# Half of the second row block's normed rows: turned by VectorE 32x32 blocks and a trip through DRAM in place of TensorE

## Chip, core and metric

One core of one Trainium2 chip runs the whole program. The metric is the device time of one execution in microseconds (us). Before the change it is 1993.98 us, the median of three runs (1991.19 to 1994.17).

## What is computed

A decoder layer on 256 tokens of width 2048, in float32: a half-step SwiGLU feed-forward (inner width 5632), a token mixer with two attention branches, a second half-step feed-forward, and a LayerNorm behind each of the three. Only the frame matters here:

```python
h = _layer_norm(ALPHA * h + 0.5 * _swiglu(h, ffn1_w_gate, ffn1_w_up, ffn1_w_down), ln1_g, ln1_b)
mix = _mixer(h, positions, w_in, ...)
h = _layer_norm(ALPHA * h + mix, ln2_g, ln2_b)
return _layer_norm(ALPHA * h + 0.5 * _swiglu(h, ffn2_w_gate, ffn2_w_up, ffn2_w_down), ln3_g, ln3_b)
```

`_layer_norm` takes each row's mean and variance over its 2048 values, and then scales and shifts each column. A matmul on TensorE contracts over partitions, so the normed rows (tokens on the partitions) have to be turned into columns (channels on the partitions) before the next projection can use them.

## The kernel before, in words

**Rows and quads.** The 256 tokens are two blocks of 128 rows, b = 0 and b = 1. The 2048 channels are 16 column tiles of 128, handled in four quads of four tiles (`q` or `c`, 0 to 3); a quad of one block is a 128 x 512 tile. `Acts` holds a turned activation as two float32r tiles, a rounded part `hi` and the rest `lo`. `split` (L148 to L150) makes them: ScalarE copies the source into `hi` (L149), and VectorE subtracts (L150). Each weight tile is loaded by SP's DMA queue and split in the same way into a ring of buffers (`wring`). A product is then three matmuls (`triple`, L202 to L204): hi x hi, hi x lo, lo x hi.

**Order of the work.** `project` (L209) runs over units of two k tiles. A unit is load, split, then 6 matmuls for block 0 and 6 for block 1. The products of block 1 lag behind those of block 0 by `lag` units (`LAG` is 5; `narrow_to` sets it to 1 and shortens the ring). `tick` counts a step per unit, and `later(n, fn)` runs `fn` n steps further on. That is the order in which the program is written; when the kernel is built, a scheduler orders each engine's instructions with its own estimates of their durations. On the chip each engine runs its list strictly in order, and an instruction that waits holds up everything behind it on its engine.

**LayerNorm 1 and 2.** In `LayerNorm.apply(b)` (L604), VectorE computes the factor of a block, then centers and scales each quad in place (L624), and `rows_to_quad` (L498) turns it: four TensorE transposes of 128 x 128 into one PSUM bank (L501), four ScalarE activations with the column's gain and shift from PSUM to SBUF (L506, into `h1raw` or `h2raw` for quads 0 and 1, which are kept for later sums, and into a temporary tile `full` for quads 2 and 3), and `x.put`, which splits. Behind it, twelve and more steps later, `finish` multiplies the rows by the gains and adds the shifts (L629, L630), and GpSimd's DMA queue writes them to DRAM as the next residual (`res<-z`, L1135). LayerNorm 1 runs where the first feed-forward's down projection ends and the mixer's first projections begin (`wc0`, 512 columns; then `narrow_to(6)`, `wc1`, 256 columns, and `wc2`, 320 columns). LayerNorm 2 runs where `w_out` ends and the second feed-forward's gate and up projection begins. In both, the products of block 1's quads 2 and 3 come last among the first projection's products.

**The other way of turning.** `turn_out` (L533) has VectorE transpose a 128 x 512 tile in 32 x 32 blocks (L536), and GpSimd's queue write it with four DMAs of 64 KB to a DRAM tile (L538), so that the blocks land in their turned places. `turn` (L544) reads the tile back with one DMA of 256 KB (L550) into `turned`, `wait` steps after it was written out, and hands it to its user `more` steps after that. In before this way is used for the feed-forward's inner activations and for several of the mixer's tensors, whose column order within a quad is made up for by a host-side order of the weight rows. `blocks`, `turned` and `full` come from one pool of six temporary tiles.

**Where the mixer's key row comes in.** Some 45 us after LayerNorm 1, VectorE makes a rotated key row per block (`kr_row`, L813 to L888), which TensorE turns (L821) amid the first sevenfold products.

Of the kernel before, what the change touches and what calls it, by code (L numbers as in the profile page):

```python
# [14 lines left out]
AF = mybir.ActivationFunctionType  # L15
# [3 lines left out]
P = 128  # L19
# [40 lines left out]
def layer_kernel(ctx: ExitStack, tc: tile.TileContext, a: dict, out: bass.AP):  # L60
    nc = tc.nc
    V, S, GP, PE = nc.vector, nc.scalar, nc.gpsimd, nc.tensor
# [9 lines left out]
    def nm(s):  # L72
        uid[0] += 1
        return f"{s}_{uid[0]}"
# [4 lines left out]
    def tmp_tile(shape, name="tmp", dt=F32):  # L79
        return small.tile(shape, dt, tag="tmp", name=nm(name), bufs=6)  # L80

    def sm(n, name="sm", dt=F32):
        return small.tile([P, n], dt, tag="sm", name=nm(name), bufs=24)
# [4 lines left out]
    def tr_bank(name="tr"):  # L88
        return psum.tile([P, 512], F32, tag="tr", name=nm(name), bufs=3)
# [13 lines left out]
    def later(n, fn):  # L103
        uid[0] += 1
        heapq.heappush(todo, (step[0] + n, uid[0], fn))
# [392 lines left out]
    def rows_to_quad(src, b, x, q, gain=None, shift=None):  # L498
        t = tr_bank()
        for i in range(4):  # L500
            PE.transpose(t[:, i * P:(i + 1) * P], src[:, i * P:(i + 1) * P], ident)  # L501
        if gain is not None:
            full = x.raw(q, b) if q in x.kept else tmp_tile([P, 512], "full")
            for i in range(4):
                k = 4 * q + i
                S.activation(full[:, i * P:(i + 1) * P], t[:, i * P:(i + 1) * P], AF.Identity,  # L506
                             bias=shift[:, k:k + 1], scale=gain[:, k:k + 1])
            t = full
        x.put(q, b, t.rearrange("p (i t) -> p i t", i=4))

    def rstd(v, eps, n, between=None):
        ve = sm(n, "ve")
        V.tensor_scalar(out=ve, in0=v, scalar1=eps, scalar2=None, op0=ALU.add)
        sd = sm(n, "sd")
        S.activation(sd, ve, AF.Sqrt, scale=4.0)
        w = sm(n, "w")
        V.tensor_scalar(out=w, in0=v, scalar1=eps, scalar2=-4.0, op0=ALU.add, op1=ALU.mult)
        if between is not None:
            between()
        y = sm(n, "y")  # L520
        V.reciprocal(y, sd)
        t = sm(n, "t")
        if n == 1:
            V.scalar_tensor_tensor(out=t, in0=y, scalar=w, in1=y, op0=ALU.mult, op1=ALU.mult)
        else:
            y2 = sm(n, "y2")
            V.tensor_tensor(out=y2, in0=y, in1=y, op=ALU.mult)
            V.tensor_tensor(out=t, in0=y2, in1=w, op=ALU.mult)
        f = sm(n, "f")
        V.scalar_tensor_tensor(out=f, in0=t, scalar=3.0, in1=y, op0=ALU.add, op1=ALU.mult)  # L530
        return f

    def turn_out(row, to):  # L533

        t = tmp_tile([P, 512], "blocks")
        V.transpose(t, row)  # L536
        for i in range(4):
            nc.gpsimd.dma_start(to.rearrange("(g r) (i f) -> i r g f", g=4, i=4)[i],  # L538
                                t[32 * i:32 * (i + 1), :].rearrange("r (g f) -> r g f", g=4))

    def turned(v):
        return v.rearrange("p (i k c) -> p k i c", i=4, k=4)

    def turn(row, use, wait, more):  # L544
        to = dram.tile([P, 512], F32, name=nm("turn"))
        turn_out(row, to)

        def back():
            t = tmp_tile([P, 512], "turned")
            nc.gpsimd.dma_start(t, to)  # L550
            later(more, lambda: use(turned(t)))
        later(wait, back)

    def turn_to_quad(row, b, x, q, wait, more):
        turn(row, lambda t: x.put(q, b, t), wait, more)

    def turn_to_cols(row, dst, b, wait, more):
        turn(row, lambda t: S.copy(dst[:, :, b * P:(b + 1) * P].rearrange("p k (i c) -> p k i c", i=4), t), wait, more)

    class LayerNorm:  # L560
        def __init__(self, scale, residual, g, bt, each, x=None, cols=None, at=((0, 2, 4, 6), (8, 11, 14, 17))):
# [42 lines left out]
        def apply(self, b):  # L604
            mv = sm(2, "mv")
            V.bn_aggr(mv, self.stats[b].rearrange("p a s -> p (a s)"))
            zs = [self.z[b][c // 2][:, (c % 2) * 512:(c % 2) * 512 + 512] for c in range(4)]
            gs, bs = ([self.gb[i][c // 2][:, (c % 2) * 512:(c % 2) * 512 + 512] for c in range(4)] for i in range(2))

            if self.cols is None:  # L610
                def center(c):
                    V.scalar_tensor_tensor(out=zs[c], in0=zs[c], scalar=mv[:, 0:1], in1=gs[c],
                                           op0=ALU.subtract, op1=ALU.mult)
                r = rstd(mv[:, 1:2], LN_EPS, 1, lambda: center(0))
                for c in range(4):
                    if c > 0:
                        center(c)
                    V.scalar_tensor_tensor(out=zs[c], in0=zs[c], scalar=r, in1=bs[c],
                                           op0=ALU.mult, op1=ALU.add)
                    self.each(b, c, zs[c])  # L620
                return
            r = rstd(mv[:, 1:2], LN_EPS, 1)
            for c in range(4):
                V.tensor_scalar(out=zs[c], in0=zs[c], scalar1=mv[:, 0:1], scalar2=r,  # L624
                                op0=ALU.subtract, op1=ALU.mult)
                rows_to_quad(zs[c], b, self.x, c, *self.cols)

            def finish(c):
                V.tensor_tensor(out=zs[c], in0=zs[c], in1=gs[c], op=ALU.mult)  # L629
                V.tensor_tensor(out=zs[c], in0=zs[c], in1=bs[c], op=ALU.add)  # L630
                self.each(b, c, zs[c])
            for c in range(4):
                later(12 + c, lambda c=c: finish(c))

    def ffn(n, x, wgu, wdn, residual, g, bt, each, first=None, between=None, nxt=None, cols=None):
# [3 lines left out]
        def put_h(b, q):  # L639
            turn_out(hb[b, q], hT[q, b])  # L640
# [103 lines left out]
    bias = [const.tile([P, 384], F32, name=f"bias{h}") for h in range(DH)]  # L744
# [105 lines left out]
    def mixer(x):  # L850
# [11 lines left out]
        def c_norm(b, i):  # L862
            c = c_row[b][:, i * RANK:(i + 1) * RANK]
            junk = tmp_tile([P, RANK], "junk")
            ss = sm(1, "ss")
            S.activation(junk, c, AF.Square, accum_out=ss)
            ms = sm(1, "ms")
            V.tensor_scalar(out=ms, in0=ss, scalar1=1.0 / RANK, scalar2=None, op0=ALU.mult)
            r = rstd(ms, RMS_EPS, 1)
            V.scalar_tensor_tensor(out=c, in0=c, scalar=r, in1=gain[:, i * RANK:(i + 1) * RANK],  # L870
                                   op0=ALU.mult, op1=ALU.mult)
            turns[i, b] = dram.tile([P, 512], F32, name=nm("turn"))
            later(2, lambda: turn_out(c, turns[i, b]))
# [23 lines left out]
        def cols_proj(w, xx, kt, name, k0=0, more=10):  # L897
            dst = act_tile([P, 4, T], F32, name)

            def done(b, bank):  # L900
                t = tmp_tile([P, 512], name + "r")
                S.copy(t, bank)
                later(1, lambda: turn_to_cols(t, dst, b, 4, more))
            project(w, xx, kt, 512, done, k0)
            return dst
# [16 lines left out]
        def pair_cols(w, name):  # L922
            dst = [act_tile([P, 4, T], F32, name) for _ in range(2)]

            def done(n, b, bank, snap, op):
                t = tmp_tile([P, 512], name + "r")
                V.tensor_tensor(out=t, in0=bank, in1=snap, op=op)
                later(1, lambda: turn_to_cols(t, dst[n], b, 4, 10))
            hy.group(w[0], w[1], done)
            return dst  # L930
# [86 lines left out]
        def qr_done(b, bank):  # L1017
            t = tmp_tile([P, 512], "qr")
            tv = t.rearrange("p (j h i) -> p j h i", j=2, h=MH)
            rope(tv[:, 0], tv[:, 1], bank, b, MH)  # L1020
            later(1, lambda: turn_to_cols(t, qrT, b, 4, 10))
# [193 lines left out]
def _build(arrays):  # L1215
    import numpy as np
    import concourse.bacc as bacc

    nc = bacc.Bacc("TRN2", target_bir_lowering=False, num_devices=1)
    aps = {k: nc.dram_tensor(f"in_{k}_dram", v.shape, mybir.dt.from_np(v.dtype), kind="ExternalInput").ap()  # L1220
           for k, v in arrays.items()}
    out = nc.dram_tensor("out_0_dram", (T, D), F32, kind="ExternalOutput").ap()
    with tile.TileContext(nc) as tc:
        layer_kernel(tc, aps, out)
    return nc
# [9 lines left out]
```

## Time and profile before

| | before |
|---|---|
| median of three runs | 1993.98 us |
| profiled execution | 1992.28 us |
| its span, first to last instruction | 1990.5 us |
| granted TensorE clock, mean | 0.998 of full |
| busy: TensorE, VectorE, ScalarE | 1975.2, 1720.4, 1229.8 us |
| GpSimd, its DMA issues above all | 255.2 us |
| DMA, mean over the span | 233 GB/s |

In the profile, PE is TensorE's matmuls (transposes on TensorE among them), PEld its weight loads, DVE VectorE, ACT ScalarE, POOL GpSimd with its DMA queue, SPq the queue of SyncE. A row of the timeline has start, duration, engine, line, operation, output and inputs, and in brackets how long the engine stood idle before and what it waited for. Durations of matmuls overlap, since they are pipelined: the distance of two starts says what one costs. Lines are those of the kernel before; behind the change the same code lies 4 to 17 lines lower.

### The profile page before, as it was taken

The numbers are of one execution on the slowest core, as the hardware profiler recorded it, in microseconds if no ns is written. First come the engines' busy times: TensorE is split into PE (matmuls) and PEld (weight loads), VectorE is DVE, ScalarE is ACT, GpSimd is POOL, SyncE is SP. The second block draws the span as 40 slices with busy tenths as digits, with TensorE's granted clock in tenths as the row PEclk, the third lists the DMA queues.
The fourth block names the chain that finished last, engine by engine and source line by source line (L and its number), as shares of the span: only waits on it lengthen the run. The fifth ranks groups of instructions, "written<-read, shape, count | busy, mean of one in ns | idle before, by whom it ended". The sixth has DMA issues, their size and how long they took to land.

```text
span 1990.5 us, 25358 instructions
## 1 busy us (share of the span) xinstructions
PE 1975.2 (99%) x8868; PEld 1635.2 (82%) x8868; DVE 1720.4 (86%) x2019; ACT 1229.8 (62%) x1548; POOL 255.2 (13%) x475
## 2 busy tenths in 40 slices
PE   9999999999999999999999999999999999999997
PEld 7888888888888897888888888888888888888886
DVE  7999999999897689999775576799999999987875
ACT  6666666666665566666675754566666666665551
POOL 0111001012110011022130130011110100121000
PEclk9999999999999999999999999999999999999999
DMA  8667756668776666676675686657776666588673
GB/s 326 217 221 267 243 195 211 216 218 264 275 267 225 211 231 235 221 253 231 220 247 187 244 281 227 221 208 238 233 281 204 204 219 234 192 284 294 221 240 110
DMA packets 134607, 463.63 MB, mean 233 GB/s; under 512 B 19616, under 2 KB 19664, under 8 KB 134480
## 3 DMA queue, kind: packets, MB, share of 16 engines
q1 hardware_dynamic: 109296, 389.59, 56.9%
q0 software_dynamic: 25184, 72.43, 11.9%
q8 instruction: 69, 1.13, 0.2%
q14 instruction: 58, 0.48, 0.1%
HBM read 433.11 MB, written 28.84 MB: 232 GB/s over the span
## 4 chain that ended last, share of the span: by engine, by line
PE 94%; DVE 3%; DMA 1%; issue 1%; ACT 0%; SPq 0%; DVEq 0%; ACTq 0%
PE mm L204 30%; PE mm L202 30%; PE mm L203 30%; DVE wring L150 1%; PE tr L202 1%; PE tr L204 1%; PE tr L203 1%; DVE sraw L344 1%; PE tr L501 0%; ACT wring L149 0%; DMA raw<-in_wc_dram 0%; DMA sraw<-in_gu_dram 0%; DMA sraw<-in_wgd_dram 0%; DMA raw<-in_gu_dram 0%; PE tr L1039 0%
## 5 line engine op out<-in xcount | busy, mean ns | idle before, releaser
L150 DVE TENSOR_TENSOR wring<-raw,wring 128x1024 fp32r<-128x1024 f32 (+2 forms) x511 | 612.8, 1204 | 171.6 <-ACT wring L149 165.7
L149 ACT CAST wring<-raw 128x1024 fp32r<-128x1024 f32 (+2 forms) x511 | 529.3, 1040 | 357.7 <-PE mm L204 253.0
L149 ACT CAST wring<-sraw 128x1024 fp32r<-128x1024 f32 x406 | 422.4, 1052 | 195.2 <-PE mm L204 102.3
L202 PE MATMUL mm<-wring,h 128*128 128x512 f32 (+2 forms) x1384 | 534.8, 387 | 0.0
L204 PE MATMUL mm<-wring,h 128*128 128x512 f32 (+2 forms) x1384 | 533.6, 386 | 0.0
L203 PE MATMUL mm<-wring,h 128*128 128x512 f32 (+2 forms) x1384 | 532.6, 385 | 0.0
L150 DVE TENSOR_TENSOR wring<-sraw,wring 128x1024 fp32r<-128x1024 f32 x406 | 487.6, 1219 | 19.2 <-ACT wring L149 14.1
L204 PEld LDWEIGHTS mm<-wring,h 128*128 128x128 f32 x1384 | 260.0, 188 | 52.8 <-DVE h L150 1.4
L203 PEld LDWEIGHTS mm<-wring,h 128*128 128x128 f32 x1384 | 260.0, 188 | 51.6 <-DVE wring L150 0.2
L202 PEld LDWEIGHTS mm<-wring,h 128*128 128x128 f32 x1384 | 260.0, 188 | 51.5 <-ACT h L149 1.0
L203 PE MATMUL mm<-wring,xs 128*128 128x512 f32 x708 | 275.6, 389 | 0.9 <-DVE wring L150 0.9
L202 PE MATMUL mm<-wring,xs 128*128 128x512 f32 x708 | 275.9, 390 | 0.5 <-ACT snap L321 0.5
L204 PE MATMUL mm<-wring,xs 128*128 128x512 f32 x708 | 275.5, 389 | 0.0
L344 DVE TENSOR_TENSOR sraw<-sraw,sraw 128x1024 f32<-128x1024 f32 x200 | 240.8, 1215 | 0.8 <-DMA sraw<-in_gu_dram 0.7
L538 POOL DMA_DIRECT2D hT<-blocks x176 | 95.7, 551 | 760.9 <-DVE blocks L536 708.5
L203 PEld LDWEIGHTS mm<-wring,xs 128*128 128x128 f32 x708 | 132.9, 188 | 28.9 <-DVE wring L150 1.4
L202 PEld LDWEIGHTS mm<-wring,xs 128*128 128x128 f32 x708 | 133.0, 188 | 28.7 <-ACT snap L321 1.0
L204 PEld LDWEIGHTS mm<-wring,xs 128*128 128x128 f32 x708 | 133.0, 188 | 27.4
L203 PE MATMUL mm<-wring,x 128*128 128x512 f32 x384 | 149.6, 390 | 0.5 <-DVE wring L150 0.5
L202 PE MATMUL mm<-wring,x 128*128 128x512 f32 x384 | 149.4, 390 | 0.4 <-ACT wring L149 0.4
L204 PE MATMUL mm<-wring,x 128*128 128x512 f32 x384 | 149.2, 389 | 0.0
L203 PEld LDWEIGHTS mm<-wring,x 128*128 128x128 f32 x384 | 72.1, 188 | 16.1 <-DVE wring L150 1.3
(266 smaller groups left out, 1888.6 us busy)
## 6 DMA issues: line engine op xcount, KB each, us to landing
raw<-in_gu_dram SPq DMA_DIRECT2D x191, 512.0 KB, 4.3
sraw<-in_gu_dram SPq DMA_DIRECT2D x160, 512.0 KB, 5.4
raw<-in_dn_dram SPq DMA_DIRECT2D x144, 512.0 KB, 4.5
hraw<-hT POOLq DMA_DIRECT2D x80, 256.0 KB, 4.9
sraw<-in_dn_dram SPq DMA_DIRECT2D x32, 512.0 KB, 5.4
raw<-in_w_out_dram SPq DMA_DIRECT2D x32, 512.0 KB, 4.4
raw<-in_wgm_dram SPq DMA_DIRECT2D x24, 512.0 KB, 4.5
raw<-in_wgd_dram SPq DMA_DIRECT2D x24, 512.0 KB, 4.2
```

Source lines behind the costliest of these rows:

```text
L149: S.copy(hi, src)
L150: V.tensor_tensor(out=lo, in0=src, in1=hi.bitcast(F32), op=ALU.subtract)
L202: PE.matmul(o, xh, wh, start=first, stop=False, skip_group_check=again)
L203: PE.matmul(o, xh, wl, start=False, stop=False, skip_group_check=again)
L204: PE.matmul(o, xl, wh, start=False, stop=last, skip_group_check=again)
L344: V.tensor_tensor(out=t, in0=t, in1=R[add[1]][s], op=ALU.add)
L538: nc.gpsimd.dma_start(to.rearrange("(g r) (i f) -> i r g f", g=4, i=4)[i], t[32 * i:32 * (i + 1), :].rearrange("r (g f) -> r g f", g=4))
```

## The change

In LayerNorm 1 and 2, quads 2 and 3 of block 1 are no longer turned by `rows_to_quad`. VectorE turns them in 32 x 32 blocks, written in a crossed order (`plain`), so that the tile that comes back holds the columns in their natural order; GpSimd's queue writes each to DRAM with four DMAs and reads it back with one, 2 steps later; and 1 step after that ScalarE applies gain and shift from the tile in SBUF, four column tiles at a time, and `x.put` splits. Block 0, and quads 0 and 1 of block 1, are turned as before. LayerNorm 3 turns nothing.

```diff
-    def turn_out(row, to):
+    def turn_out(row, to, plain=False):
         t = tmp_tile([P, 512], "blocks")
-        V.transpose(t, row)
+        if plain:
+            V.transpose(t.rearrange("p (k g f) -> p g k f", k=4, g=4), row.rearrange("p (g k r) -> p g k r", g=4, k=4))
+        else:
+            V.transpose(t, row)
...
-    def turn(row, use, wait, more):
+    def turn(row, use, wait, more, plain=False):
         to = dram.tile([P, 512], F32, name=nm("turn"))
-        turn_out(row, to)
+        turn_out(row, to, plain)
...
+    def turn_to_scaled(row, b, x, q, gain, shift, wait, more):
+        def use(v):
+            full = tmp_tile([P, 512], "full")
+            for i in range(4):
+                k = 4 * q + i
+                S.activation(full[:, i * P:(i + 1) * P].rearrange("p (i c) -> p i c", i=4), v[:, i], AF.Identity,
+                             bias=shift[:, k:k + 1], scale=gain[:, k:k + 1])
+            x.put(q, b, full.rearrange("p (i t) -> p i t", i=4))
+        turn(row, use, wait, more, True)
...
-                rows_to_quad(zs[c], b, self.x, c, *self.cols)
+                if b == 1 and c >= 2:
+                    turn_to_scaled(zs[c], b, self.x, c, *self.cols, 2, 1)
+                else:
+                    rows_to_quad(zs[c], b, self.x, c, *self.cols)
```

## The prediction

> **What bounds the kernel now.** I read the page first (busy times, then the chain that ended last), and then each engine's timeline where the two LayerNorms turn block 1.
>
> ```profile
> span 1990.5 us, 25358 instructions
> PE 1975.2 (99%) x8868; PEld 1635.2 (82%) x8868; DVE 1720.4 (86%) x2019; ACT 1229.8 (62%) x1548; POOL 255.2 (13%) x475
> ...
> PE 94%; DVE 3%; DMA 1%; issue 1%; ACT 0%; SPq 0%; DVEq 0%; ACTq 0%
> ```
>
> PE is busy 99% of the span and holds 94% of the chain. So a PE instruction that goes is worth its own time at most, and a wait that PE gets costs its full length. Everything else counts only where PE waits for it.
>
> ```profile
> L501 PE MATMUL tr<-ident,z x64: 270/273/328, 692.1 to 1303.5; 128*128 128x128 f32 x64
> ...
> 704.38 0.39 PE L202 MATMUL mm<-wring,h 128*128 128x512 f32 x1
> 704.61 1.47 PE L501 MATMUL tr<-ident,z 128*128 128x128 f32 x12
> 705.84 0.48 PE L203 MATMUL mm<-wring,h 128*128 128x512 f32 x1
> ...
> 706.39 0.40 PE L202 MATMUL mm<-wring,h 128*128 128x512 f32 x1
> ...
> 706.80 0.66 PE L501 MATMUL tr<-ident,z 128*128 128x128 f32 x4
> ...
> 707.22 0.48 PE L203 MATMUL mm<-wring,h 128*128 128x512 f32 x1
> ...
> 718.69 0.28 PE L202 MATMUL mm<-wring,h 128*128 128x256 f32 x1
> 718.80 0.28 PE L203 MATMUL mm<-wring,h 128*128 128x256 f32 x1
> ```
>
> The first row counts the normed rows' transposes: 64, sixteen per block and LayerNorm, of which 48 are left. The others are LayerNorm 1, block 1. Starts tell the cost: a 512-wide matmul takes 0.23 us (704.38 to 704.61), a 256-wide one 0.12. The sixteen transposes stand in two groups, twelve (1.23 us to the next matmul) and four.
>
> **What goes.** Eight of the sixteen: four of the group of twelve, 4/12 x 1.23 = 0.41 us, and the group of four with the wait ahead of it, 707.22 - 706.39 - 0.23 = 0.60 us. That is 1.0 us in LayerNorm 1. LayerNorm 2:
>
> ```profile
> 1301.55 1.85 ACT L506 ACTIVATE h2raw<-tr,cols 128x128 f32<-128x128 f32 x5 [4.21 <-PE tr L501]
> ...
> 1303.27 0.63 ACT L149 CAST h<-h2raw 128x512 fp32r<-128x512 f32 x1
> ...
> 1302.69 0.40 PE L203 MATMUL mm<-wring,h 128*128 128x512 f32 x1
> 1303.11 0.66 PE L501 MATMUL tr<-ident,z 128*128 128x128 f32 x4
> 1303.52 0.47 PE L204 MATMUL mm<-wring,h 128*128 128x512 f32 x1
> 1303.96 0.50 PE L202 MATMUL mm<-wring,h 128*128 128x512 f32 x1
> ```
>
> The same 1.0 us goes from PE (0.41, and 1303.52 - 1302.69 - 0.23 = 0.60). But the matmul at 1303.96 is block 1's first, and it starts 0.06 us after ScalarE has split quad 0 (1303.27 + 0.63 = 1303.90). ScalarE's five activations and that split stay as they are in the built order, so PE would only wait 1.0 us longer: **gain 0**. In LayerNorm 1 it is otherwise: its split of quad 0 ends at 707.6,
>
> ```profile
> 706.97 0.64 ACT L149 CAST h<-h1raw 128x512 fp32r<-128x512 f32 x1
> ...
> 703.83 1.91 DVE L624 TENSOR_SCALAR z<-z,mv,f 128x512 f32<-128x512 f32 x4
> ```
>
> and PE, with eight transposes (0.82 us) and the nine matmuls that the built order still puts ahead, is there at 704.61 + 0.82 + 9 x 0.23 = 707.5. The gain holds: 1.0.
>
> **What comes.** Per LayerNorm: two VectorE transposes, eight writes and two reads on POOL's queue, and ScalarE's eight activations and two splits, now from `turned` and later in its order.
>
> ```profile
> L536 DVE STREAM_TRANSPOSE blocks<-c_row x4: 699/702/707, 722.2 to 759.2; 128x512 f32<-128x512 f32 x4
> ...
> L538 POOL DMA_DIRECT2D turn<-blocks x104: 548/548/567, 723.2 to 1173.2; - x104
> ...
> DMA to landing us min/median/max: 1.9/2.5/6.3
> ...
> L550 POOL DMA_DIRECT2D turned<-turn x22: 546/567/572, 871.5 to 1178.1; - x22
> ...
> DMA to landing us min/median/max: 2.9/4.2/6.3
> ```
>
> The first landing line is that of the 64 KB writes, the second that of the 256 KB reads. The crossed write is in no row of before; I take the plain one's 0.70 us; the bounds are nothing more, and twice that (each run of 32 elements written apart), which would put quad 0's `lo` 1.4 us later and cost PE as much in each LayerNorm. The Trainium skill's page "DMA: Bandwidth & Descriptors", section "Anatomy of one DMA — SWDGE (gpsimd) path", gives 2.0 us plus the bytes at 436 GB/s, so 2.15 and 2.6 us by its figures as an estimate; the reads above land later than that, and by the page LayerNorm 1's loss below would shrink by some 0.6 us.
>
> LayerNorm 1, by medians. Rows are normed at 703.83 + 1.91 = 705.74; `blocks` are ready at 706.4 and 707.1; POOL issues 706.4 to 710.8 (8 x 0.55). The last write of quad 2, issued at 708.05, has landed at 710.6, so its read goes out at 710.8 and lands at 715.0. POOL then puts two residual writes ahead of quad 3's read (issue 712.8, landing 717.0). ScalarE, in its new order, first casts two `wc1` units that wait for ring buffers which PE still holds:
>
> ```profile
> 709.37 1.55 ACT L506 ACTIVATE full<-tr,cols 128x128 f32<-128x128 f32 x4
> ...
> 712.30 0.67 ACT L876 COPY c_row<-mm 128x512 f32<-128x512 f32 x1
> ...
> 713.28 0.73 ACT L866 ACTIVATE junk<-c_row 128x512 f32<-128x512 f32 x1
> ...
> 713.91 0.71 ACT L149 CAST wring<-raw 128x512 fp32r<-128x512 f32 x1
> ```
>
> PE does 35 matmuls from 705.4 (713.8 with 0.2 us for quad 0's `lo`, which now stands behind two transposes on VectorE), then 24 of `wc1`, 256 wide. The second of these two units can only be cast when PE has let its buffer go (714.0), so its `lo` comes at 715.35 and PE loses 0.4. PE reaches quad 2 at 717.15; ScalarE has it scaled and split by 715.0 + 1.4 + 0.6 = 717.0, in time. Quad 3: `c_row` to 717.6, scaled to 719.0, `junk` with its read-out to 719.9, split 720.5. PE is due after 12 matmuls at 719.9: 0.6 lost. The next `wc1` cast stands behind all that: 0.35. The waits sum to 0.2 + 0.4 + 0.6 + 0.35 = **1.5 us**, against 1.0 gained: +0.5. With the shortest landings, 1.9 and 2.9, the last two waits go (0.6 lost, -0.4 in all); with the longest, 6.3 and 6.3, the trip is 5.9 us longer and nearly all of that is PE's.
>
> LayerNorm 2, by medians. Normed at 1302.1, `blocks` 1302.8 and 1303.5, POOL 1302.8 to 1307.2; reads at 1307.3 and (after quad 3's last write, issued at 1306.7) 1309.2, landing at 1311.5 and 1313.4. The lag of five units is still on, and the built order has 46 matmuls between 1303.96 and quad 2, 63 before its second half: due at 1314.4 and 1318.3. ScalarE first casts a unit whose buffer PE lets go at about 1310.8, so it begins at 1311.8: scaled and split at 1311.8 + 2.0 = 1313.8. For quad 3, with a table load and a gate's activation in between,
>
> ```profile
> 1308.81 1.28 ACT L645 ACT_TABLE_LOAD   x1
> 1310.11 0.39 ACT L645 ACTIVATE sg<-mm 128x256 f32<-128x256 f32 x1
> ```
>
> 1313.4 + 1.4 + 1.28 + 0.39 + 0.6 = 1317.1. Both have about 1 us to spare (the trip 0.9, quad 3's 1.2): loss 0, up to 5.0 with the longest landings.
>
> **What is behind it.** VectorE's 2.8 us of new transposes have to find slack:
>
> ```profile
> 704.00:712.00 8.00, 7.98 (x44) 6.42 (x43) 8.00 (x15) 6.75 (x19) 2.24 (x5) 1.00 0.42 159
> 712.00:720.00 8.00, 8.00 (x40) 6.74 (x39) 6.25 (x15) 5.10 (x12) 0.54 (x1) 1.00 0.55 178
> ...
> 736.00:744.00 8.00, 8.00 (x56) 8.00 (x56) 4.53 (x5) 4.34 (x5) 0.00 (x0) 1.00 1.03 415
> ...
> 752.00:760.00 8.00, 7.17 (x32) 5.31 (x32) 8.00 (x21) 4.77 (x9) 2.17 (x4) 1.00 0.37 100
> ...
> 1315.00:1325.00 10.00, 10.00 (x45) 8.17 (x44) 7.60 (x9) 3.81 (x6) 0.54 (x1) 1.00 0.86 305
> ...
> 752.53 0.40 PE L204 MATMUL mm<-wring,xs 128*128 128x512 f32 x1
> 753.76 0.33 PE L821 MATMUL tr<-ident,kr_row 128*128 128x128 f32 x1 [0.83 <-DVE kr_row L816]
> ```
>
> After the length of the stretch come PE, PEld, DVE, ACT. VectorE stands idle 1.75 us in 712 to 720, 3.5 in 736 to 744, 2.4 in 1315 to 1325: the cover is there. At 752.76 PE waits 1.0 us for the key row. The built order moves that transpose behind other matmuls, but VectorE is full there (8.00 of 8), so what PE does not wait here it may wait one instruction further on. Between -1.0 and +1.0, I take 0. SP's queue has the same loads, some in another order; no wait of PE on them shows here, so 0.
>
> **Sum**: -1.0 + 1.5 + 0 + 0 = +0.5 us on the profiled execution of 1992.28 us (its span and 1.8 us around it). The median of the runs is 1.7 us above that execution, so I add the 0.5 to the median, 1993.98: 1994.5 us.
>
> **Rivals.** (1) *The new waits don't come.* Trips at their shortest and the key row's wait gone: -0.4 - 1.0 = -1.4, about 1992.6. For it: ScalarE idles 2.9 of 8 us in 712 to 720. Against it: in-order casts that hang on PE's own progress.
> (2) *ScalarE is held by the trip* (slower). Quad 2's first activation waits for the read, and behind it on ScalarE stand all weight casts. In LayerNorm 1 every us by which the trip is longer than by medians counts, in LayerNorm 2 what is over 0.9. I count it from 3 us on: 0.5 + 3 + 2.1 = +5.6, about 2000; at the longest landings 0.5 + 5.9 + 5.0 = +11.4, about 2005. For it: two DMAs in a row, one of which POOL must see landed, and residual writes in the same queue.
> (3) *POOL is kept from making its descriptors.* If each issue had to wait for a VectorE instruction as long as the transpose (0.70 us), ten issues would shift the trip by 7.0 us, and the LayerNorms would lose 7.0 + 6.1: about 2008. Against it: VectorE is busy all of 704 to 712, and POOL's residual writes there took no longer than elsewhere and landed as fast:
>
> ```profile
> L1135 POOL DMA_DIRECT2D res<-z x8: 539/539/552, 698.3 to 713.3; - x8
> ...
> DMA to landing us min/median/max: 2.3/2.4/4.3
> ```
>
> That rule is the Trainium skill's, page "SBUF — State Buffer", section "Who interferes with whom": VectorE's two-port modes lock GpSimd out of a shared port pair. By these rows the trace does not show it here.
>
> **How the numbers follow.** Forecast 0.55; (1) 0.18; (2) 0.20; (3) 0.04; a gain of over 4 us, for which the 2.0 us of removed transposes and 1.0 us of the key row don't suffice, 0.03. Two tenths of a per cent, 4 us, is about what a measurement of this kernel can tell from no change. The forecast and (1) lie within it, (2) and (3) outside. Faster 0.03, same 0.73, slower 0.24. The range: down to 1991.0, for (1) and the spread of the runs; up to 2000.0, for the forecast's open ends (trips up to 3 us longer, the crossed write) and the near end of (2).
>
> **What would show it.** In the profile after: L501 with 48 instructions on `z`; PE's first matmul of block 1 in LayerNorm 2 still at ScalarE's split of quad 0; `full<-turned` on ScalarE idle before it for DMA `turned<-turn`, by nothing in LayerNorm 2 and under 1 us in LayerNorm 1; PE waits of some 1.5 us in the 15 us behind LayerNorm 1's transposes. I am wrong if the `turned` reads land later than 5 us after issue, if the crossed transpose takes over 1 us, or if waits of PE grow far behind these places.

## The result, and the profile after

The changed kernel takes 1997.3 us (median of 13 runs, 1995.77 to 2001.0); the kernel before, in runs beside it, 1993.33 us (13 runs, 1990.31 to 1994.61). The ratio is 1.0022, with a 95% interval of 1.0015 to 1.003: about 4.4 us slower, just over the 4 us that the forecast's "same" reached to, and inside the range. The page of the changed kernel, its first lines and the chain's shares by engine:

```profile
span 1995.4 us, 25347 instructions
PE 1975.2 (99%) x8852; PEld 1632.0 (82%) x8852; DVE 1722.7 (86%) x2023; ACT 1232.6 (62%) x1548; POOL 266.1 (13%) x495
...
PE 91%; DVE 4%; DMA 2%; ACT 1%; issue 1%; POOL 0%; SPq 0%; DVEq 0%; ACTq 0%; POOLq 0%
```

The span is 4.9 us longer (1990.5 before). PE has 16 instructions less, and 3% of the chain has gone from PE to VectorE, DMA and ScalarE: that is what PE now waits for. Where the 4.9 us arise is read from starts that both traces have: PE's first transpose of a normed row (L501 on `z`, LayerNorm 1), the first product of the differential attention (`tr<-dkT,dqT`), its first transpose on `diff`, and the end. Columns are durations (min/median/max), then the first and the last start. Before:

```profile
L964 PE MATMUL tr<-dkT,dqT x32: 270/327/382, 956.9 to 1017.2; 128*128 128x128 f32 x16, 128*128 128x256 f32 x16
...
L501 PE MATMUL tr<-ident,diff x16: 272/272/273, 1189.7 to 1205.0; 128*128 128x128 f32 x16
```

After:

```profile
L981 PE MATMUL tr<-dkT,dqT x32: 270/327/382, 960.9 to 1021.4; 128*128 128x128 f32 x16, 128*128 128x256 f32 x16
...
L501 PE MATMUL tr<-ident,z x48: 270/272/300, 692.3 to 1306.7; 128*128 128x128 f32 x48
...
L501 PE MATMUL tr<-ident,diff x16: 270/272/273, 1194.7 to 1210.0; 128*128 128x128 f32 x16
```

| stretch | before | after | longer by |
|---|---|---|---|
| start to LayerNorm 1's first transpose | 692.1 | 692.3 | 0.2 |
| from there to the first attention product | 264.8 | 268.6 | **3.8** |
| on to the first transpose on `diff` | 232.8 | 233.8 | 1.0 |
| on to the end (LayerNorm 2 lies here) | 800.8 | 800.7 | -0.1 |

So LayerNorm 1 and the 260 us behind it pay nearly all, LayerNorm 2 nothing. What PE waited for, in the whole execution (total, times, longest), before and then after:

```profile
PE mm L203 <- DVE wring L150: 1.4, 2, 0.9
...
PE tr L821 <- DVE kr_row L816: 0.8, 1, 0.8
```

```profile
PE mm L203 <- DVE wring L150: 4.4, 6, 1.4
PE mm L202 <- ACT h L149: 2.3, 3, 1.1
```

The larger part is not the turned quads (`h`) but weights whose second part VectorE had not subtracted yet (`wring`). PE's timeline has these waits at

```profile
743.16 0.42 PE L203 MATMUL mm<-wring,h 128*128 128x320 f32 x1 [0.26 <-DVE wring L150]
...
761.21 0.50 PE L203 MATMUL mm<-wring,xs 128*128 128x512 f32 x1 [1.37 <-DVE wring L150]
...
798.83 0.50 PE L203 MATMUL mm<-wring,xs 128*128 128x512 f32 x1 [0.97 <-DVE wring L150]
...
928.12 0.50 PE L203 MATMUL mm<-wring,xs 128*128 128x512 f32 x1 [1.03 <-DVE wring L150]
```

that is 25, 45, 80 and 210 us behind the trip. (The one near 798 is in before too, 0.85 us at 796.47. Whether the one at 928 belongs to the price is taken up under `again`.) How it comes about stands on ScalarE's timeline in LayerNorm 1:

```profile
713.65 0.62 ACT L149 CAST wring<-raw 128x512 fp32r<-128x512 f32 x1 [0.74 <-PE mm L204]
714.41 1.65 ACT L569 ACTIVATE full<-turned,cols 128x128 f32<-128x128 f32 x4
716.10 0.62 ACT L149 CAST h<-full 128x512 fp32r<-128x512 f32 x1
...
718.20 1.65 ACT L569 ACTIVATE full<-turned,cols 128x128 f32<-128x128 f32 x4 [1.00 <-DMA turned<-turn]
...
720.38 0.60 ACT L149 CAST h<-full 128x512 fp32r<-128x512 f32 x1
...
720.99 1.12 ACT L149 CAST wring<-raw 128x512 fp32r<-128x512 f32 x2
```

Between the cast at 713.65 and that at 720.99, ScalarE casts no weight for 7.3 us. Only 1.0 us of that is idle; the rest is work that comes late because the reads do: scaling and splitting the two quads, which before was over at 713.5, and `c_row` and `junk` behind it. Before, ScalarE cast weights in that time, at 713.91 and then at

```profile
714.62 0.60 ACT L149 CAST wring<-raw 128x512 fp32r<-128x512 f32 x1
715.49 0.63 ACT L149 CAST wring<-raw 128x512 fp32r<-128x512 f32 x1 [0.26 <-PE mm L204]
716.85 0.62 ACT L149 CAST wring<-raw 128x512 fp32r<-128x512 f32 x1 [0.73 <-PE mm L204]
718.21 0.62 ACT L149 CAST wring<-raw 128x512 fp32r<-128x512 f32 x1 [0.74 <-PE mm L204]
```

VectorE, which subtracts behind each cast, has nothing to do, and PE waits for quad 3:

```profile
720.50 0.15 DVE L885 TENSOR_SCALAR ms<-ss 128x1 f32<-128x1 f32 x1 [3.06 <-ACT junk L883]
```

```profile
721.03 0.50 PE L202 MATMUL mm<-wring,h 128*128 128x512 f32 x1 [0.97 <-ACT h L149]
```

A raw weight buffer comes free when VectorE has subtracted, and only then SP can load the next tile into it. Before, SP sent five such loads from 716.0 to 721.7; in the changed kernel it sends none between 715.1 and 722.4:

```profile
L229 SPq DMA_DIRECT2D raw<-in_wc_dram x5: 327/328/328, 716.0 to 721.7; - x5
```

```profile
722.39 0.33 SPq L229 DMA_DIRECT2D raw<-in_wc_dram  x1
```

The first load of the gate weights behind the projections (`in_wgm_dram`, first start), which stands in SP's queue right behind such loads, goes out 3.6 us later than before, while PE is only 1.3 us late at that point (its first 320-wide matmul starts at 732.2, before at 730.9). Before and after:

```profile
L339 SPq DMA_DIRECT2D sraw<-in_wgm_dram x8: 327/382/1045, 730.6 to 766.7; - x8
```

```profile
L339 SPq DMA_DIRECT2D sraw<-in_wgm_dram x8: 328/447/729, 734.2 to 769.1; - x8
```

The stretches tell the rest (length; PE, PEld, DVE, ACT, POOL busy; clock; DMA share, GB/s):

```profile
712.00:720.00 8.00, 8.00 (x47) 6.64 (x45) 3.78 (x7) 5.80 (x13) 3.02 (x6) 1.00 0.91 287
...
744.00:752.00 8.00, 8.00 (x46) 7.21 (x45) 7.41 (x17) 5.93 (x11) 0.00 (x0) 1.00 1.03 418
...
760.00:768.00 8.00, 6.79 (x30) 5.55 (x31) 8.00 (x9) 5.68 (x8) 2.17 (x4) 1.00 0.43 103
```

VectorE was busy 6.25 of 8 us in the first of them before and is busy 3.78 now, with more work to do in the program: the idle time that I had counted as cover for its transposes grew. The burst of loads that stood in 736 to 744 (415 GB/s) now stands in 744 to 752 (418 GB/s), and by 760 VectorE is full and PE waits for it.

### The profile page after: what moved, and what is told of

Read it like the earlier page. It is cut to its first block, busy times and chain, and to the rows that moved or that the text cites. A ratio compares the mean times of both kernels' runs of the same rounds, so it can differ in the third digit from the quotient of the medians.

```text
span 1995.4 us, 25347 instructions
## 1 busy us (share of the span) xinstructions
PE 1975.2 (99%) x8852; PEld 1632.0 (82%) x8852; DVE 1722.7 (86%) x2023; ACT 1232.6 (62%) x1548; POOL 266.1 (13%) x495
## 4 chain that ended last, share of the span: by engine, by line
PE 91%; DVE 4%; DMA 2%; ACT 1%; issue 1%; POOL 0%; SPq 0%; DVEq 0%; ACTq 0%; POOLq 0%
PE mm L203 29%; PE mm L204 29%; PE mm L202 29%; DVE wring L150 2%; PE tr L204 1%; PE tr L203 1%; PE tr L202 1%; DVE sraw L344 0%; ACT wring L149 0%; POOL turn L542 0%; DMA turn<-blocks 0%; DMA raw<-in_wgm_dram 0%; DMA sraw<-in_wgd_dram 0%; DMA raw<-in_gu_dram 0%; DMA turned<-turn 0%
## 5 line engine op out<-in xcount | busy, mean ns | idle before, releaser
L542 POOL DMA_DIRECT2D turn<-blocks x120 | 65.4, 552 | 162.3 <-DVE blocks L540 114.3
```

## The experiments

Ratios are to runs of the kernel before beside them, with 95% intervals. Theory A: ScalarE's list is held by the two scaled quads, and what PE loses is the weights behind them. Its rivals stand in the expectations.

| kernel | median, us | before beside it | ratio (interval) |
|---|---|---|---|
| `again` | 1998.61 | 1992.61 | 1.0027 (1.0016 to 1.0037) |
| `ln1` | 1996.94 | 1992.61 | 1.0020 (1.0011 to 1.0029) |
| `ln2` | 1998.06 | 1992.61 | 1.0027 (1.0017 to 1.0037) |
| `unturned` | 1991.2 | 1992.61 | 0.9995 (0.9986 to 1.0004) |
| `idle_trip` | 1993.34 | 1993.04 | 1.0000 (0.9990 to 1.0009) |
| `no_trip` | 1992.11 | 1993.04 | 0.9989 (0.9979 to 0.9998) |
| `more2` | 1996.59 | 1993.04 | 1.0017 (1.0007 to 1.0026) |
| `first` | 2000.59 | 1993.04 | 1.0035 (1.0023 to 1.0047) |
| `hold` | 1996.24 | 1993.11 | 1.0016 (1.0007 to 1.0025) |
| `quad3` | 1998.55 | 1993.11 | 1.0027 (1.0017 to 1.0036) |
| `ln2_again` | 1998.98 | 1993.11 | 1.0028 (1.0018 to 1.0039) |
| `ln2_shifted` | 1994.15 | 1992.08 | 1.0010 (1.0001 to 1.0019) |

**again**: the changed kernel, unchanged.

> The changed kernel once more, for a second profile. Theory A (ScalarE's queue is held by the two scaled quads in LayerNorm 1; weight buffers come free late, and TensorE pays far behind): 1997.3 +- 1 us, and the waits of TensorE near 721 (1.1 us), 761 (1.5 us) and 928 us (1.2 us) come again, with at most 0.5 us of change each. Rival B (the waits far behind, at 928 and 1037 us, are scatter of one execution): the time stays, but these two, 1.8 us together, are missing or stand elsewhere.

The waits come again at 721 (1.5 us idle) and 761 us (1.1); that at 928 is 0.3 us here, with another of 0.6 at 946. The stretch from LayerNorm 1's first transpose to the first attention product is 269.0 us (692.2 to 961.2), so 4.2 longer than before: its total is no scatter, but which load PE meets late is in part. Rival B is right about the single waits far behind. That near 1037 is gone, and one at the place of 928 comes also in kernels that cost nothing, here in `idle_trip`:

```profile
924.09 0.50 PE L203 MATMUL mm<-wring,xs 128*128 128x512 f32 x1 [0.24 <-DVE wring L150]
```

`ln1`, which follows, pays the whole stretch without it: its trace names no wait of PE between 801 and 960 us. The waits for `orow` (near 1038) and `diff` (near 1208) come in some profiles and not in others, of kernels with and without the change; the stretch behind the attention products is left open for that reason.

**ln1** and **ln2**: the change in one LayerNorm alone (in `ln2` the name is "h2").

```diff
-                if b == 1 and c >= 2:
+                if b == 1 and c >= 2 and self.x.name == "h1":
```

> The change in LayerNorm 1 alone. Theory A: nearly all of the 4 us, about 1997 us; the profile shows the waits near 721, 743 and 761 us again and TensorE about 4 us late by 1100 us. Rival C (LayerNorm 2 has the larger share: its reads through DRAM landed 5 us after issue and ScalarE's second quad was late): about 1995 us.

> The change in LayerNorm 2 alone. Theory A: within 0.5 us of before, about 1993.5 us: TensorE waits 1.25 us for quad 0's split (0.22 before), loses 0.4 us at quad 3, and the wait of 0.7 us at 1354 us goes. Rival C: about 1995.5 us.

LayerNorm 1 alone costs what the change costs, 4.3 us. Its rows, with the first transpose at 692.3:

```profile
L981 PE MATMUL tr<-dkT,dqT x32: 270/327/382, 960.9 to 1021.2; 128*128 128x128 f32 x16, 128*128 128x256 f32 x16
...
L501 PE MATMUL tr<-ident,diff x16: 270/272/273, 1194.0 to 1209.4; 128*128 128x128 f32 x16
```

268.6 us in the stretch, as in the changed kernel. But LayerNorm 2 alone costs 5.4 us, where theory A expected 1993.5 us and rival C 1995.5: both missed, and the two LayerNorms together cost less than the sum. Its profile has the cost where it should not be, behind 1190.5 (1996.2 - 1190.5 = 805.7 us to the end, before 800.8):

```profile
1318.57 0.50 PE L202 MATMUL mm<-wring,h 128*128 128x512 f32 x1 [3.01 <-ACT h L149]
...
1324.31 0.50 PE L202 MATMUL mm<-wring,h 128*128 128x512 f32 x1 [1.59 <-ACT h L149]
```

VectorE's and POOL's rows say why: VectorE's two transposes, then POOL's eight writes, and the landing of the two reads.

```profile
1302.86 1.30 DVE L538 STREAM_TRANSPOSE blocks<-z 128x512 f32<-128x512 f32 x2
```

```profile
1306.44 4.37 POOL L542 DMA_DIRECT2D turn<-blocks  x8 [4.25 <-DVE z L647]
```

```profile
DMA to landing us min/median/max: 5.3/5.8/6.2
```

The first block was ready at 1303.6, and in the changed kernel POOL starts 0.3 us after it (1307.04 + 0.71, then 1308.05). Here it starts 2.9 us after it. The releaser that the view names, `z`, is an instruction that the write doesn't need. With reads that land late as well, the trip is far over LayerNorm 2's slack of 1 us. What keeps POOL is taken up below.

**unturned**: quads 2 and 3 of block 1 are scaled but not turned.

```diff
-                    turn_to_scaled(zs[c], b, self.x, c, *self.cols, 2, 1)
+                    full = tmp_tile([P, 512], "full")
+                    for i in range(4):
+                        k = 4 * c + i
+                        S.activation(full[:, i * P:(i + 1) * P], zs[c][:, i * P:(i + 1) * P], AF.Identity,
+                                     bias=self.cols[1][:, k:k + 1], scale=self.cols[0][:, k:k + 1])
+                    self.x.put(c, b, full.rearrange("p (i t) -> p i t", i=4))
```

> Quads 2 and 3 of block 1 in both LayerNorms are scaled straight from the normed rows, so they are not turned at all (this leaves out that part of the computation): TensorE's 16 transposes go and nothing comes. It measures what they are worth. Theory of the prediction (1.0 us in LayerNorm 1, nothing in LayerNorm 2): about 1992.3 us. Rival D (a built order that moves with any edit here costs as much as the trip does): 1995 us or more. Rival E (both LayerNorms gain their 1.0 us): about 1991.3 us.

1.4 us by the medians, with an interval of 2.8 us faster to 0.8 us slower: all that TensorE's sixteen transposes can give is less than a measurement tells. In its profile PE again meets ScalarE's split of quad 0 in LayerNorm 2 (a wait of 1.09 us at 1302.78), so what gain there is lies in LayerNorm 1. The time alone is rival E's 1991.3, but the kernel before was faster in these runs too, and the interval holds the prediction's 1.0 us as well as E's 2.0. Rival D, that any edit here costs through a moved order, falls.

**idle_trip** and **no_trip** divide the trip from those who wait for it. In `idle_trip` TensorE turns everything and the trip's result is dropped:

```diff
-                    turn_to_scaled(zs[c], b, self.x, c, *self.cols, 2, 1)
+                    turn(zs[c], lambda t: None, 2, 1, True)
+                    rows_to_quad(zs[c], b, self.x, c, *self.cols)
```

> TensorE turns all four quads as before, and the trip (two crossed VectorE transposes, eight writes, two reads per LayerNorm) runs beside it with nobody using what it brings back. Theory A (the price comes from ScalarE waiting, in order, for the reads): within 0.7 us of before, about 1993 us. Rival F (the price is the work itself: VectorE's 2.8 us, POOL's issues and the extra transfers): 1996 us or more.

In `no_trip`, ScalarE scales the blocks where VectorE wrote them, which leaves out the moves between partitions, so that these quads hold other values:

```diff
-                    turn_to_scaled(zs[c], b, self.x, c, *self.cols, 2, 1)
+                    t = tmp_tile([P, 512], "blocks")
+                    V.transpose(t.rearrange("p (k g f) -> p g k f", k=4, g=4), zs[c].rearrange("p (g k r) -> p g k r", g=4, k=4))
+                    def use(v, c=c):
+                        full = tmp_tile([P, 512], "full")
+                        for i in range(4):
+                            k = 4 * c + i
+                            S.activation(full[:, i * P:(i + 1) * P].rearrange("p (i c) -> p i c", i=4), v[:, i], AF.Identity,
+                                         bias=self.cols[1][:, k:k + 1], scale=self.cols[0][:, k:k + 1])
+                        self.x.put(c, b, full.rearrange("p (i t) -> p i t", i=4))
+                    later(3, lambda t=t, use=use: use(turned(t)))
```

> The crossed transposes stay, but ScalarE scales quads 2 and 3 straight from the blocks that VectorE wrote, so the part of the turning that the DRAM trip does is left out. Theory A: without a read to wait for, ScalarE's casts come as early as before and TensorE keeps what the missing transposes gave it, as when nothing was turned: 1991.5 to 1993 us. Rival F (VectorE's transposes cost): 1995 us or more.

The first costs nothing (1.0000, 0.9990 to 1.0009), the second gains 0.1%. VectorE's transposes, POOL's issues and the transfers are hidden, as the prediction had them; the price comes only where ScalarE uses what they bring. Without that the loads go out as before, here in `no_trip`:

```profile
L339 SPq DMA_DIRECT2D sraw<-in_wgm_dram x8: 327/386/1034, 729.6 to 765.1; - x8
```

**hold** puts the wait back, but not the need: TensorE turns all quads and uses them, and ScalarE scales what the trip brings into a tile that nobody reads (`drop`: the four activations of `use` above, into a spare `full`, and no `put`).

```diff
-                    turn_to_scaled(zs[c], b, self.x, c, *self.cols, 2, 1)
+                    turn(zs[c], drop, 2, 1, True)
+                    rows_to_quad(zs[c], b, self.x, c, *self.cols)
```

> TensorE turns all four quads as before and uses those; the trip runs beside it, and ScalarE scales what it brings back into a tile that nobody reads (eight more activations per LayerNorm, 3.3 us of ScalarE, and its wait for the reads). Theory A (weight casts that stand behind the wait on ScalarE come late, and TensorE pays for them far behind LayerNorm 1): 1995 to 1998 us, with waits of TensorE on casts between 715 and 765 us though its quads are there. Rival H (TensorE pays only because quads 2 and 3 themselves are late): within 1 us of before, about 1993.5 us.

3.1 us slower, by theory A. ScalarE waits, with no weight cast for 5.3 us (718.18 to 723.45), and the first gate load goes out at 733.9:

```profile
718.18 0.60 ACT L149 CAST wring<-raw 128x512 fp32r<-128x512 f32 x1
721.28 1.65 ACT L645 ACTIVATE full<-turned,cols 128x128 f32<-128x128 f32 x4 [2.49 <-DMA turned<-turn]
...
723.45 0.60 ACT L149 CAST wring<-raw 128x512 fp32r<-128x512 f32 x1
```

```profile
PE mm L203 <- DVE wring L150: 4.5, 8, 1.4
```

PE's waits for `wring` sum to what they do in the changed kernel (4.4 us in 6), though they stand elsewhere (1.33 us at 730.21, 0.24 at 762.77), and there is none for `h`, since the quads are there. The stretch from LayerNorm 1's first transpose to the first attention product is 268.7 us, as long as in the changed kernel (268.6); in `idle_trip` it is 264.8, as before, and in `no_trip` 264.2. So the late quad is not needed for the loss; a held ScalarE is enough. Of the 5.3 us in `hold`, 2.5 are waiting and 1.65 an activation group that the kernel before doesn't have; no run has these activations (3.3 us per LayerNorm) without the wait, so the two are not told apart.

**more2** brings the scaled quads one unit later in the program (`*self.cols, 2, 2`).

> The changed kernel, but the scaled quads come one unit later in program order (2 units after the read is issued, not 1), so that in LayerNorm 1 the quads' activations stand behind c_row's and between weight casts. Theory A: ScalarE no longer waits for the reads, the weight casts between come earlier; TensorE waits less at 721 us and 761 us: 1994 to 1996 us. Rival G (what counts is when the quads are there, not what ScalarE casts meanwhile): no better than the change, 1997 to 1999 us.

3.5 us slower, 0.6 above theory A's range and 0.4 below the rival's; the premise failed. The quads' activations moved behind `junk`, not behind the weight casts: ScalarE waits 1.85 us at 718.75 for quad 3 and has cast no weight from 713.99 to 720.30, and the first gate load goes out at 734.0. It tells nothing against theory A or for G.

**first** norms and turns quads 2 and 3 of block 1 ahead of 0 and 1.

```diff
-            for c in range(4):
+            for c in ((0, 1, 2, 3), (2, 3, 0, 1))[b]:
```

> The changed kernel, but in block 1 quads 2 and 3 are normed and turned ahead of quads 0 and 1, so both trips begin about 1 us earlier and quad 0 comes about 2.2 us later. Theory A: the reads land 1 us earlier and ScalarE holds the casts 1 us less, but TensorE, which waits for quad 0 in LayerNorm 2 already, loses 2 us there: 1996 to 1999 us. Rival G: quads 2 and 3 earlier alone count, 1995 us or less.

Slower by 0.35%, 1.6 us above theory A's range. Both LayerNorms now wait for quad 0: PE 1.54 us in LayerNorm 1 (711.27), 1.00 and 2.00 us in LayerNorm 2 (1307.01 and 1310.11). That ScalarE no longer waits for a read at all (its activations at 716.00 and 718.58 stand idle for nothing) does not make up for it; the weight casts come late all the same, with none between 717.55 and 721.75.

**quad3** lets one quad take the trip (`c == 3` in place of `c >= 2`).

> Only quad 3 of block 1 takes the trip, in both LayerNorms. Its four writes have no others ahead of them on POOL's queue, so the read goes out about 2 us earlier, and ScalarE has one read less to wait for; TensorE keeps half of the gain. Theory A: no hold is left in LayerNorm 1: 1992.5 to 1994 us. Rival G (any quad that comes by DRAM delays the casts): 1995 us or more.

5.4 us slower, in the range of rival G. I had reckoned with an order that the built program does not have: with one quad, the scheduler puts the crossed transpose behind four of VectorE's residual products and a split, at 710.15, though the rows are normed at 707.2; the read goes out at 716.8, lands 4.6 us later, and ScalarE stands 2.93 us. The wait is longer with half of the work. That fits theory A, but my expectation was wrong, and this run doesn't tell A from G; `idle_trip` and `hold` do that.

**ln2_again** and **ln2_shifted** settle POOL's late start.

> The change in LayerNorm 2 alone, a second profile. In the first, POOL issued the first write 2.6 us after the blocks were there, the reads took 5.3 and 6.2 us to land, and TensorE waited 3.2 and 1.8 us for the two quads. Theory A as it stands (LayerNorm 2 has 1 us of slack, and what the trip takes beyond it is paid in full): the waits at 1318 and 1324 us follow the issue and landing times of this profile; if POOL issues at once and the reads land in 4 to 5 us, both waits are under 1 us together. Rival I (the late issue belongs to this build): POOL is 2.6 us late again and the time is 1997 to 1998 us again.

It belongs to the build: the blocks are ready at 1303.3, POOL starts at 1306.18, as late as the first time, and 1998.98 us, 1 us more than rival I had. Counting POOL's DMAs, this write is the 326th. In other kernels, where POOL has nothing else to wait for, the 220th, the 326th and the 432nd stand idle as long, whatever they are. In the changed kernel the 220th is the fifth of eight writes that otherwise follow each other without a gap, and the 432nd the second of the eight writes of an `hT` block:

```profile
924.21 2.17 POOL L542 DMA_DIRECT2D turn<-blocks  x4 [2.17 <-DVE wring L150]
...
1716.84 3.79 POOL L542 DMA_DIRECT2D hT<-blocks  x7 [2.47 <-issue]
```

and in `quad3` the 326th, a load of the bias vector amid others:

```profile
1193.28 1.08 POOL L594 DMA_DIRECT2D gb<-in_ln_b_dram  x2 [2.31 <-issue]
```

In the changed kernel the trip in LayerNorm 1 adds ten DMAs ahead of it, so the 326th is a load at 1186.9 and hurts nobody; without those ten it is the trip's first write in LayerNorm 2. `ln2_shifted` tests that: the change in LayerNorm 2, and `idle_trip`'s two lines in LayerNorm 1, so that the count is the same again.

> The change in LayerNorm 2; in LayerNorm 1 TensorE turns all quads and the trip runs beside it unused, so that POOL's queue holds 486 DMAs, as in the changed kernel. Theory J (POOL pauses about 2.3 us ahead of its 220th, 326th and 432nd DMA, whatever they are; in the kernel with the change in LayerNorm 2 alone the 326th is the trip's first write, here it is a load near 1187 us): the first write goes out 0.3 us after its blocks, TensorE waits under 1 us for quads 2 and 3 together, and the time is within 1 us of before, about 1993.5 us. Rival I (the change in LayerNorm 2 without that in LayerNorm 1 costs its 5 us in any case): 1997 to 1999 us.

POOL starts at 1304.88, 0.3 us after its blocks; the reads are waited for 0.83 us, PE waits 0.50 us for quad 3 and nothing for quad 2, and from the first transpose on `diff` to the end it takes 1992.5 - 1191.5 = 801.0 us, 800.8 before and 805.7 in `ln2`:

```profile
1304.88 4.36 POOL L542 DMA_DIRECT2D turn<-blocks  x8 [1.68 <-DVE blocks L538]
```

```profile
L501 PE MATMUL tr<-ident,diff x16: 270/272/273, 1191.5 to 1206.9; 128*128 128x128 f32 x16
```

Of the 5.4 us, 2.1 are left (0.2 to 3.8 by the interval), more than the 1 us expected; in its profile the 2.0 us that the span is longer stand ahead of 1191.5, where of the change only LayerNorm 1's unused trip runs, but that is one execution. That LayerNorm 2's trip is harmless when POOL issues at once is shown for its own stretch; that nothing at all is left is not.

## Why the prediction was right, and where it was wrong

The range held the time, and the sign of the sum (+0.5) was that of the result. The size was not: +4.4 us. Both hits are in part luck. The sum was positive only by 0.6 us of waits that did not come. The upper part of the range was meant for trips up to 3 us longer and for the crossed write, while the trips came within 1.5 us of the forecast and the write cost nothing more. And two of the prediction's own signs of being wrong came: waits of PE far behind the places it named, and a read that landed later than 5 us. Point by point:

- **Transposes gone, 1.0 us in LayerNorm 1 and nothing in LayerNorm 2.** As forecast: `unturned` gains little (-1.4 us, the interval reaching over 0), and PE's first matmul of block 1 in LayerNorm 2 still starts with ScalarE's split of quad 0, in the changed kernel 0.05 us behind it (1308.30 + 0.63):

```profile
1308.30 0.63 ACT L149 CAST h<-h2raw 128x512 fp32r<-128x512 f32 x1
```

```profile
1308.98 0.50 PE L202 MATMUL mm<-wring,h 128*128 128x512 f32 x1 [1.09 <-ACT h L149]
```

- **The crossed write costs as much as the plain one.** 0.69 us, the plain one 0.70; the upper bound falls:

```profile
L538 DVE STREAM_TRANSPOSE blocks<-z x4: 671/692/711, 705.9 to 1307.7; 128x512 f32<-128x512 f32 x4
```

- **The trip in LayerNorm 1.** Reads forecast at 710.8 and 712.8, landing 4.2 us later; they went out at 711.2 and 713.3, and landed 3.1 and 4.8 us later, quad 3 thus 1.1 us late. In LayerNorm 2 they took 3.2 and 5.4 us.

```profile
L554 POOL DMA_DIRECT2D turned<-turn x2: 553/562/572, 711.2 to 713.3; - x2
...
DMA to landing us min/median/max: 3.1/4.0/4.8
```

All reads of these trips, in all kernels here, took 3.0 to 6.2 us. The Trainium skill's page "DMA: Bandwidth & Descriptors", section "Anatomy of one DMA — SWDGE (gpsimd) path", gives about 2.0 us and the bytes at 436 GB/s for one DMA, an estimate of 2.6 us for such a read; no read here was that short. The prediction had LayerNorm 1's loss shrink by 0.6 us with that estimate; by its own sum for the shortest landings (1.9 and 2.9 us, about as long together) the loss shrinks to 0.6, that is by 0.95.
- **The waits beside the trip, 1.5 us.** Of its four terms, the 0.2 for quad 0 and the 0.4 for a `wc1` unit did not come, and quad 3 with the cast behind it, 0.6 + 0.35, came as one wait of 0.97 us at 721.03. That the two agree is luck: it is 1.50 us in `again`.
- **LayerNorm 2, loss 0.** Right in the changed kernel: 0.56 us of ScalarE for quad 3, 0.27 of PE, and the stretch no longer than before. Right by luck of the count, as `ln2` shows.
- **The key row, 0 with 1.0 either way.** Its wait of 0.83 us went in the changed kernel. But `ln2` and `ln2_again`, the same kernel, have 0 and 0.59 us there, so that its going is scatter; and the 1.37 us at 761.21 are no other place of the same wait, for `idle_trip`, where the key row's wait is gone too, has none there.
- **What is behind it: VectorE's cover, and "SP's queue has the same loads [...] so 0". This step failed.** I costed the weights that stand behind the wait on ScalarE at 0.35 us, the next cast alone, and looked at VectorE's idle time as room. But ScalarE's cast, VectorE's subtraction and SP's next load form one loop through the raw buffers. ScalarE's list held for 7.3 us put all of it some 3.6 us back, PE used up the lead it had, and then paid at 743 and 761 us. `hold` shows that the hold does it without a late quad, `idle_trip` and `no_trip` that without the hold nothing of it is left. Of the 3.8 us in the stretch, rows name 3.0. Each wait is counted here by starts, from the last matmul before it to the second behind it, less two undisturbed steps (at 721.03: 721.37 - 719.68 - 0.46 = 1.23, where the idle column, which counts from a modelled end, has 0.97). So the waits at 721, 743, 761 and 928 cost 1.23, 0.53, 1.63 and 1.30 us and that near 798 0.12 more than before; the key row's 1.0 and 0.8 for eight transposes go off. The other 0.8 I could not place, and how much of the 1.30 the change brings is open.
- **Rival 1** (the new waits don't come) missed: quad 3's came in each profile of the changed kernel, and in `ln1` (1.55 us).
- **Rival 2** had the right mechanism, ScalarE held by the trip with the weight casts behind it, and counted it only from trips longer than by medians. It should have counted the hold itself.
- **Rival 3** (POOL kept from its descriptors by VectorE) did not come: in the changed kernel, `ln2` and `ln2_shifted` the eight writes took 4.36 to 4.37 us beside a busy VectorE, 0.55 us each. The Trainium skill's page "SBUF — State Buffer", section "Who interferes with whom", has VectorE's two-port modes block GpSimd; no run here shows that. POOL's pause in `ln2` goes with the count of DMAs, not with what VectorE does: in the changed kernel the same list of VectorE instructions runs at that place and POOL does not pause.

No version here that computes the whole beats the kernel before by more than its measurement tells (`no_trip`, which leaves out the moves, gains 0.1%); the most that could be had from these transposes is what `unturned` shows.

## What to carry to other kernels

Where an engine that prepares the bound engine's operands waits in order for a DMA, count everything of the loop behind it: casts not done are buffers not freed and loads not sent, and the bound engine pays when its lead is used up, here at the wait itself and 25 to 45 us later. Idle time of the engine next in that loop was no cover here, for it was idle because of the wait. And put the cheapest test first: the added work with nobody waiting for it, and the wait with nobody needing it, tell in two runs which of them costs.

## What the runs showed of the hardware that I had not expected

POOL's DMA queue stood idle 2.2 to 2.5 us ahead of its 220th, 326th and 432nd DMA in the places quoted, where nothing in the trace that it waits for is late; these are 106 apart, whatever the DMAs' size and direction (64 KB writes, 512 KB loads). The pause goes with the count of DMAs and not of instructions: the 326th is POOL's 480th, 484th or 485th instruction in the changed kernel, `quad3` and `ln2`. It is not seen every 106 DMAs: the 114th stands behind a gap of 13.6 us in every kernel, where no pause can be told, the 8th goes out without a gap, and in `no_trip` the 432nd follows 1.7 us behind the one before. In kernels where something else holds the queue at that count, no pause of its own can be seen. What it does in that time, no run here shows. Adding DMAs to the queue thus moves the pause to another place: in `ln2` onto the write for which TensorE then waited 4.6 us in two waits.
